# Two column passes joined into one in the MLP's seven-product units of a float32 decoder trunk

## The chip, the cores and the metric

The kernel runs on one core of a Trainium2 chip. A core has a matrix engine (TensorE, PE in the profile; its weight loads are PEld), VectorE (DVE), ScalarE (ACT), GpSimd (POOL) and SyncE (SP, which issues most transfers here). SBUF is the working memory, PSUM the banks into which PE writes and from which DVE and ACT read. The metric is the device time of one execution in microseconds (us), as the median of several runs.

## The reference

A two-layer decoder trunk in float32, 512 tokens of width 1024, batch 1. Layer 0 mixes tokens with a gated recurrence and pooling, layer 1 with a convolution module. Each layer then has cross-attention into 256 memory tokens and the gated MLP below, each with a residual add, and a final norm ends it.

```python
def conv_ffn(x, norm, w_up, dw_w, dw_b, w_down):
    h = rms_norm(x, norm) @ w_up              # 1024 -> 2 * 3072
    g = causal_dwconv(h[..., :D_FF], dw_w, dw_b)   # width 3
    u = h[..., D_FF:]
    return (jax.nn.gelu(g) * u) @ w_down      # 3072 -> 1024

for layer in range(DEPTH):
    x = x + mixer(x)                          # one kind in layer 0, another in layer 1
    x = x + cross_attn(x, mem, ...)
    x = x + conv_ffn(x, ...)
return rms_norm(x, final_norm)
```

## The kernel before

Activations lie transposed: a tile is 128 channels by 512 tokens (`T`), and X is eight such tiles. Float32 products are made of rounded parts: each operand is split into a high part (a copy by ACT into the type float32r) and a low part (what is left, a subtraction by DVE), and `mm3` (L186 to L188) runs three matmuls: high weights by high input, high weights by low input, low weights by high input. For one pair of tiles this is called a k-step below, and each matmul a pass.

In each layer's MLP the up projection has 24 units, numbered 0 to 23. Units 0 and 1 are plain. Units 2 to 23 each make one tile of the gate and one of the value by a scheme of seven products instead of eight (Strassen's in Winograd's form): weights and input are cut in 2 x 2 blocks, the tokens into two halves of 256 (`M`). `Seven` holds the input's side: the blocks B11, B21, B22 are halves of the normed input's tiles (`norm.x[c]`, a high and a low tile of 512 columns each; columns 0 to 255 of tiles 0 to 3 are B11, of tiles 4 to 7 B21, and columns 256 to 511 of tiles 4 to 7 are B22), and T1 to T4 are sums of blocks kept in eight `big` tiles, high and low apart. `Blocks` holds the weights' side: a11, a12, a22 as loaded, and s1 to s4, which are made by accumulating DMAs on POOL's queue (L825, L828, L830), then split by `high` (ACT, L815) and `low` (DVE, L822). `Seven.product` makes one product: four k-steps, so twelve passes of 256 columns.

A unit accumulates in three PSUM tiles, each a bank of which columns 0 to 255 are used. All come from the pool `main_ps` with five banks. `stat_ps` has one bank, `aux_ps` two.

- H: s1 by T1, then s4 by B22
- G: a11 by B11, then a12 by B21
- F: starts as ACT's copy of G after a11 by B11 (L928), then s2 by T2, s3 by T3, a22 by T4

On PE the order in unit c is: s1 (H), s2 (F), a12 (G), s3 (F), the down projection's 24 passes of 512 columns for an earlier group of four units, a11 of unit c + 1 (`ahead`), s4 (H), a22 (F). Partial results are read between them: u is F after s2 (ACT, L946) and F after s3 (ACT, L967); `times_r` (L887) reads G and F and multiplies by the norm's scale r; the adds of L171 read H. `gating(c)` is a generator that runs on into unit c + 1: the add of H, the multiplication by r (L905), the convolution (ACT L895, two on DVE at L898), gelu (ACT L900), the product with the value (DVE L914), and the split of the result (ACT L917, DVE L919).

The order of PE, ACT, DVE and POOL in the MLP is written out by hand (`manual_schedule`): each works through its queue in the program's order. Between the units' parts the queues of ACT and DVE also hold the splits of the next units' weights, the down weights (ACT L200, DVE L203), and ACT's copies of X into the down projection's banks and back (L855, L860); SP loads each unit's raw weights two or three units ahead. After layer 0's last unit the last group's down products are made outside a hand-written order: there a scheduler takes instructions by priority, `high_priority(n)` moves them up, and each `sum` adds into X (L866) and feeds the next norm's sum of squares (ACT L246, DVE L248), among the splits of coming weights (L166, L167).

Of the kernel before, what the change touches and what calls it, by code (L numbers as in the profile page):

```python
# [10 lines left out]
F32 = mybir.dt.float32  # L11
F32R = mybir.dt.float32r
AF = mybir.ActivationFunctionType
# [25 lines left out]

KE = 2  # L40
PARKED = 4
READY = 8
WINDOWS = (2, 4, 8, 16)

# [17 lines left out]
def trunk(ctx: ExitStack, tc: tile.TileContext, I: dict, out: list):  # L62
# [26 lines left out]
    def big_f():  # L89
        return big.tile([P, 2 * T], F32, tag="big", name=nm("big"))  # L90
# [93 lines left out]
    def mm3(ps, w, x, first, last, onto=False):  # L184
        (wh, wl), (xh, xl) = w, x
        PE.matmul(ps, wh, xh, start=first, stop=False, skip_group_check=onto)  # L186
        PE.matmul(ps, wh, xl, start=False, stop=False, skip_group_check=onto)  # L187
        return PE.matmul(ps, wl, xh, start=False, stop=last, skip_group_check=onto)  # L188
# [16 lines left out]
    def blk(w, i, n=P):  # L205
        hi, lo = (w.hi, w.lo) if isinstance(w, Piece) else w
        if isinstance(hi, list):
            hi, lo, i = hi[i // T], lo[i // T], i % T
        return hi[:, i : i + n], lo[:, i : i + n]


    class Norm:
        due = None
# [516 lines left out]
    class Seven:  # L730
# [6 lines left out]
        def __init__(self, norm, n=4):  # L737
            self.norm = norm
            self.t = [(big_r(), big_r()) for _ in range(n)]
            self.t4 = None if n == 4 else big_f()  # L740

        def fourth(self, k):
            split(self.t4[:, k * M : (k + 1) * M], *[x[:, M:] for x in self.norm.x[k]])

        def sums(self, k, between=None):

            f = [tmp_f(), tmp_f()]
            for i in range(2):
                c = k + 4 * i
                A.activation(f[i], X[c], AF.Copy, scale=col(self.norm.gain[0], self.norm.gain[1] + c))  # L750
            if between:
                between()
            (b11, b12), (b21, b22) = [(x[:, :M], x[:, M:]) for x in f]
            t13, t24 = tmp_f(), tmp_f()
            t1, t3, t2, t4 = t13[:, :M], t13[:, M:], t24[:, :M], t24[:, M:]
            V.tensor_tensor(t3, b22, b12, op=ALU.subtract)
            V.tensor_tensor(t1, b11, b12, op=ALU.subtract)
            V.scalar_tensor_tensor(t2, t3, -1.0, b11, op0=ALU.mult, op1=ALU.subtract)
            at = slice(k * M, (k + 1) * M)
            if self.t4 is not None:  # L760
                t4 = self.t4[:, at]
            V.scalar_tensor_tensor(t4, t2, -1.0, b21, op0=ALU.mult, op1=ALU.subtract)
            for (hi, _), t in zip(self.t, (t1, t2, t3, t4)):
                A.activation(hi[:, at], t, AF.Copy)
            yield
            for (hi, lo), t in zip(self.t, (t1, t2, t3, t4)):
                V.tensor_tensor(lo[:, at], t, hi[:, at].bitcast(F32), op=ALU.subtract)

        def product(self, ps, w, j, first=True):
            for c in range(4):  # L770
                if j - self.T1 == len(self.t):
                    x = blk(self.norm.x[c], M, M)
                elif j >= self.T1:
                    x = blk(self.t[j - self.T1], c * M, M)
                else:
                    x = blk(self.norm.x[c if j == self.B11 else c + 4], M if j == self.B22 else 0, M)
                mm3(ps, blk(w, c * P), x, first and c == 0, c == 3, not first)
            return ps

    class Blocks:  # L780
# [54 lines left out]
    def ffn(layer, norm, nxt, seven, pairs):  # L835
# [50 lines left out]
        def times_r(out, ps, at):  # L886
            V.tensor_tensor(out[:, at], ps, norm.r[:, at], op=ALU.mult)  # L887
# [3 lines left out]
        def gate_conv(c, g):  # L891
# [8 lines left out]
            A.activation(y, y, AF.Gelu_apprx_tanh)  # L900
            yield y

        def gating(c, g, f, u, F, H):
            add(g[:, right_half], H, u[:, :M])
            V.tensor_tensor(g[:, right_half], g[:, right_half], norm.r[:, right_half], op=ALU.mult)  # L905
# [12 lines left out]
            yield  # L918
            V.tensor_tensor(ys[c][1], y, ys[c][0].bitcast(F32), op=ALU.subtract)  # L919
# [3 lines left out]

        def ahead(c):

            G, F = main_ps()[:, :M], main_ps()[:, :M]
            m(c, G, "a11", seven.B11)
            A.activation(F, G, AF.Copy)  # L928
            return G, F

        def unit(c):

            nonlocal left, chains
            G, F = chains
# [11 lines left out]
            A.activation(u[:, :M], F, AF.Copy)  # L946
# [20 lines left out]
            A.activation(u[:, M:], F, AF.Copy)  # L967
# [6 lines left out]
            V.tensor_tensor(f[:, right_half], f[:, right_half], norm.r[:, right_half], op=ALU.mult)  # L974
            both(c + 2, "a11")
            high(c + 1, "a12")
            low(c + 1, "a12")
            if down:
                for ks in (range(GC - 1), (GC - 1,)):
                    for i in range(2):  # L980
                        down.products(i, d[i], seeded, ks)
            if c + 3 in pairs:
                pairs[c + 3].load()
            if c + 2 in pairs and c > first:
                pairs[c + 2].load_second()
            if c > second and c + 1 in downs:
                downs[c + 1].w.high()
                downs[c + 1].w.low()
            if c + 2 in downs and first < c <= CF - 2:
                downs[c + 2].load()  # L990
            high(c + 1, "s1")
            low(c + 1, "s1")
            high(c + 1, "s2")
            low(c + 1, "s2")
            if c == second:
                downs[c + 1].w.high()
                downs[c + 1].w.low()
            if down:
# [105 lines left out]
        if nxt:  # L1104
            mem = Memory(1)
            mem.operand(0)
            mem.operand(1)
            mem.outputs()
            parked = []
            for n in range(PARKED):  # L1110
                if n + 1 < C // 2:
                    downs[CF + n + 1].w = load_w(I["wdown"][(layer * NG + NG - 1) * (C // 2) + n + 1])
                parked.append(mem.key_piece(n, park=True))
            for j in range(C // 2):
                for i in range(2):
# [785 lines left out]
```

## Time and profile before

| what | value |
|---|---|
| median of 3 runs | 1429.62 us (1429.07 to 1431.03) |
| the profiled execution | 1429.09 us |
| its span, first to last instruction | 1427.3 us |
| granted TensorE clock, mean | 0.998 |
| PE busy | 1417.0 us, 8650 matmuls |
| DVE busy | 1073.2 us, 1796 instructions |
| ACT busy | 901.6 us, 1592 instructions |
| POOL busy | 317.3 us, 333 instructions |

Times of instructions are from the profiled execution and count from the start of its span. A row of a timeline gives start, duration, engine, line, operation, output and inputs by the program's names, shape and count; in brackets stands the engine's idle time before it and what ended it. The starts of neighbouring matmuls tell what each one costs, as their durations overlap.

### The profile page before, as it was taken

Reading aid. Unit: us, or ns where it says so; the run is one execution under the profiler, and the core shown is the slowest. Engines: PE = TensorE matmul, PEld = TensorE weight load, DVE = VectorE, ACT = ScalarE, POOL = GpSimd, SP = SyncE. Lnnn points to the kernel's source line nnn. Section 1 sums busy time; section 2 is a strip of 40 time slices with the busy share of each in tenths; the row PEclk is TensorE's granted clock in tenths of the full one; section 3 lists DMA queues with packets and bytes.
Section 4 is the critical chain, followed back from the end, with each engine's and each line's share of the span. In section 5 each row is a group of like instructions: output and inputs, shape, how many; then the busy total and the mean of one; then the engine's idle time right before and its main releaser. Section 6 shows DMA issues by size and latency. Waiting matters only on the chain.

```text
span 1427.3 us, 22834 instructions
## 1 busy us (share of the span) xinstructions
PE 1417.0 (99%) x8650; PEld 1262.6 (88%) x8650; DVE 1073.2 (75%) x1796; ACT 901.6 (63%) x1592; POOL 317.3 (22%) x333
## 2 busy tenths in 40 slices
PE   9999999999999999999999999999999999999998
PEld 8988888998999999999988777899889999999997
DVE  6987776778786676667798997968788676676665
ACT  7678754667565666666665557767665665666664
POOL 0011310210122222222008992011002222222211
PEclk9999999999999999999999999999999999999999
DMA  8522232544487777777442354345438777777741
GB/s 304 196 79 99 89 122 78 118 111 148 96 199 171 170 172 167 172 168 165 133 133 89 119 159 152 106 88 141 118 83 199 180 175 167 170 174 165 175 120 60
DMA packets 80031, 204.33 MB, mean 143 GB/s; under 512 B 9008, under 2 KB 9520, under 8 KB 79920
## 3 DMA queue, kind: packets, MB, share of 16 engines
q1 hardware_dynamic: 50832, 150.15, 33.0%
q0 software_dynamic: 28800, 52.44, 21.4%
q8 instruction: 68, 1.11, 0.3%
q14 instruction: 43, 0.35, 0.1%
q10 hardware_dynamic: 288, 0.27, 0.1%
HBM read 145.16 MB, written 2.10 MB: 103 GB/s over the span
## 4 chain that ended last, share of the span: by engine, by line
PE 91%; DVE 3%; POOL 2%; ACT 1%; DMA 1%; issue 1%; SPq 0%; POOLq 0%; DVEq 0%; ACTq 0%
PE mm L186 22%; PE mm L187 22%; PE mm L188 22%; PE aux L186 7%; PE aux L187 7%; PE aux L188 7%; PE mm L458 2%; DVE wlo L167 1%; DMA raw<-in_wv 1%; POOL actf L1501 1%; ACT whi L166 1%; PE aux L532 0%; POOL act L167 0%; POOL tmp L1322 0%; DMA raw<-in_pw 0%
## 5 line engine op out<-in xcount | busy, mean ns | idle before, releaser
L187 PE MATMUL mm<-act,whi 128*128 128x512 f32 (+2 forms) x1061 | 369.2, 348 | 0.3 <-DVE act L181 0.2
L186 PE MATMUL mm<-act,whi 128*128 128x512 f32 (+2 forms) x1061 | 368.8, 349 | 0.6 <-ACT act L274 0.6
L188 PE MATMUL mm<-act,wlo 128*128 128x512 f32 (+2 forms) x1061 | 368.9, 348 | 0.0
L186 PEld LDWEIGHTS mm<-act,whi 128*128 128x128 f32 x1061 | 200.5, 189 | 28.1 <-ACT act L274 1.0
L187 PEld LDWEIGHTS mm<-act,whi 128*128 128x128 f32 x1061 | 200.7, 189 | 27.4 <-DVE act L167 1.0
L188 PEld LDWEIGHTS mm<-act,wlo 128*128 128x128 f32 x1061 | 200.7, 189 | 24.9 <-DVE wlo L167 0.6
L822 DVE TENSOR_TENSOR bigr<-raw,bigr 128x512 fp32r<-128x512 f32 x176 | 120.9, 688 | 129.3 <-ACT bigr L815 125.6
L186 PE MATMUL mm<-bigr,bigr 128*128 128x256 f32 x704 | 199.4, 283 | 0.0
L187 PE MATMUL mm<-bigr,bigr 128*128 128x256 f32 x704 | 199.2, 283 | 0.0
L188 PE MATMUL mm<-bigr,bigr 128*128 128x256 f32 x704 | 199.2, 283 | 0.0
L815 ACT ACTIVATE bigr<-raw 128x512 fp32r<-128x512 f32 x176 | 109.4, 623 | 80.0 <-DVE wlo L203 75.7
L828 POOL DMA_DIRECT2D raw<-wa x100 | 87.9, 899 | 308.5 <-DVE bigr L822 208.6
L186 PE MATMUL aux<-act,whi 128*128 128x512 f32 x399 | 155.7, 390 | 0.0
L187 PE MATMUL aux<-act,whi 128*128 128x512 f32 x399 | 155.7, 390 | 0.0
L188 PE MATMUL aux<-act,wlo 128*128 128x512 f32 x399 | 155.2, 389 | 0.0
L166 ACT ACTIVATE whi<-raw 128x1024 fp32r<-128x1024 f32 (+1 forms) x95 | 96.6, 1021 | 85.2 <-PE mm L187 44.4
L186 PEld LDWEIGHTS mm<-bigr,bigr 128*128 128x128 f32 x704 | 135.1, 192 | 0.0
L188 PEld LDWEIGHTS mm<-bigr,bigr 128*128 128x128 f32 x704 | 135.2, 192 | 0.0
L187 PEld LDWEIGHTS mm<-bigr,bigr 128*128 128x128 f32 x704 | 135.2, 192 | 0.0
L825 POOL DMA_DIRECT2D raw<-raw x50 | 43.3, 866 | 367.5 <-DVE wlo L822 343.8
L167 DVE TENSOR_TENSOR wlo<-raw,whi 128x1024 fp32r<-128x1024 f32 (+1 forms) x75 | 90.4, 1211 | 19.1 <-ACT whi L166 18.5
L188 PEld LDWEIGHTS aux<-act,wlo 128*128 128x128 f32 x399 | 74.9, 188 | 15.9
(353 smaller groups left out, 3044.0 us busy)
## 6 DMA issues: line engine op xcount, KB each, us to landing
raw<-wa POOLq DMA_DIRECT2D x150, 256.0 KB, 3.4
wa<-in_wpair SPq DMA_DIRECT2D x88, 256.0 KB, 3.7
raw<-in_wpair SPq DMA_DIRECT2D x44, 512.0 KB, 3.8
big<-in_wdown SPq DMA_DIRECT2D x42, 512.0 KB, 4.5
raw<-raw POOLq DMA_DIRECT2D x50, 256.0 KB, 3.7
raw<-in_pw SPq DMA_DIRECT2D x24, 512.0 KB, 3.4
raw<-in_win SPq DMA_DIRECT2D x20, 512.0 KB, 3.3
raw<-in_wk SPq DMA_DIRECT2D x16, 512.0 KB, 3.5
```

What stands on the lines that cost most here:

```text
L166: A.activation(hi, src, AF.Copy)
L167: fetched[1] = (eng or V).tensor_tensor(lo, src, hi.bitcast(F32), op=ALU.subtract)
L186: PE.matmul(ps, wh, xh, start=first, stop=False, skip_group_check=onto)
L187: PE.matmul(ps, wh, xl, start=False, stop=False, skip_group_check=onto)
L188: return PE.matmul(ps, wl, xh, start=False, stop=last, skip_group_check=onto)
L458: PE.matmul(p, m[j], x, start=k == 0 and j == 0 and x is hi, stop=k == C - 1 and x is lo)
L815: A.activation(self.w[name][0], self.block(name), AF.Copy)
L822: V.tensor_tensor(lo, self.block(name), hi.bitcast(F32), op=ALU.subtract)
L825: G.dma_start(self.r, self.z, accum_op=ALU.add)
L828: G.dma_start(block, self.a22, accum_op=ALU.add)
L1501: G.tensor_tensor(z[:, s:], z[:, s:], f[:, s:], op=ALU.add)
```

## The change

In units 6 to 21 of each layer (`WIDE`), the products of the chains G and F run each k-step as two passes. The input's high and low parts lie side by side in one tile of 512 columns. One pass multiplies the high weights by both, into all 512 columns of the bank; the other multiplies the low weights by the high part, into the left half. The bank's right half then holds high by low, and `gather` adds the halves: ACT copies the right half out, DVE adds the left half from PSUM. H keeps three passes of 256 and takes its bank from `stat_ps` in these units. `gating` multiplies g and f by r over 512 columns at once, after the gathers. In the last k-step of a product the narrow pass comes first.

T1 to T4 are laid out side by side from the start. B11, B21 and B22 are re-laid by ACT in units 4 and 5: `put_aside` copies B22's high part out of the way, and `put_beside` moves the low parts of B11 and of B21 beside their high parts and B22's high part beside its low part, each four copies of 256 columns. In unit 7's `ahead` one more pass of 512 columns writes F's bank before ACT's copy. After layer 0's last unit the sums into X get a higher priority.

```diff
+WIDE = range(6, 22)
...
+    def parts(x):
+        return x[:, :M], x[:, M:]
+
+    def move(to, x):
+        A.activation(to, x.bitcast(F32), AF.Copy)
...
-            for (hi, _), t in zip(self.t, (t1, t2, t3, t4)):
-                A.activation(hi[:, at], t, AF.Copy)
+            both = [self.both(self.T1 + j, k) for j in range(len(self.t))]
+            for x, t in zip(both, (t1, t2, t3, t4)):
+                A.activation(x[:, :M], t, AF.Copy)
             yield
...
+        def both(self, j, c):
+            if j >= self.T1:
+                return self.t[j - self.T1][c // 2][:, c % 2 * T : (c % 2 + 1) * T]
+            return self.norm.x[c if j == self.B11 else c + 4][j == self.B22]
...
+        def put_aside(self):
+            self.aside = act_r(), act_r()
+            for c in range(4):
+                move(parts(self.aside[c // 2])[c % 2], self.norm.x[c + 4][0][:, M:])
+
+        def put_beside(self, j):
+            for c in range(4):
+                if j == self.B22:
+                    move(self.norm.x[c + 4][1][:, :M], parts(self.aside[c // 2])[c % 2])
+                else:
+                    hi, lo = self.norm.x[c if j == self.B11 else c + 4]
+                    move(hi[:, M:], lo[:, :M])
+            self.beside.add(j)
 
         def product(self, ps, w, j, first=True):
             for c in range(4):
...
+                wh, wl = blk(w, c * P)
+                if ps.shape[-1] == T:
+                    x = self.both(j, c)
+                    steps = [(ps, wh, x), (ps[:, :M], wl, x[:, :M])]
+                    for i, (to, part, by) in enumerate(steps if c < 3 else steps[::-1]):
+                        PE.matmul(
+                            to, part, by, start=first and c == 0 and i == 0, stop=c == 3 and i == 1, skip_group_check=True
+                        )
                 else:
...
+                    mm3(ps, (wh, wl), self.block(j, c), first and c == 0, c == 3, not first)
...
+        def bank(c):
+            return main_ps() if wide(c) else main_ps()[:, :M]
+
+        def gather(out, ps):
+            A.activation(out, ps[:, M:], AF.Copy)
+            add(out, ps[:, :M], out)
...
         def gating(c, g, f, u, F, H):
             add(g[:, right_half], H, u[:, :M])
-            V.tensor_tensor(g[:, right_half], g[:, right_half], norm.r[:, right_half], op=ALU.mult)
+            if wide(c):
+                V.tensor_tensor(g, g, norm.r, op=ALU.mult)
...
-            times_r(f, F, left_half)
+            if wide(c):
+                gather(f[:, left_half], F)
+                V.tensor_tensor(f, f, norm.r, op=ALU.mult)
...
         def ahead(c):
-            G, F = main_ps()[:, :M], main_ps()[:, :M]
+            G, F = bank(c), bank(c)
             m(c, G, "a11", seven.B11)
+            if c == WIDE[0] + 1:
+                PE.matmul(F, pairs[c].w["a11"][0][:, :P], seven.both(seven.B11, 0), start=True, stop=True)
             A.activation(F, G, AF.Copy)
...
-            H = main_ps()[:, :M]
+            H = (stat_ps if wide(c) else main_ps)()[:, :M]
...
             m(c, F, "s2", seven.T2, False)
+            if wide(c):
+                gather(u[:, :M], F)
...
             low(c, "s4")
-            if c > second:
+            if wide(c):
+                gather(g[:, left_half], G)
+            elif c > second:
                 times_r(g, G, left_half)
 
             m(c, F, "s3", seven.T3, False)
+            if wide(c):
+                gather(u[:, M:], F)
...
-            V.tensor_tensor(f[:, right_half], f[:, right_half], norm.r[:, right_half], op=ALU.mult)
+            if not wide(c):
+                V.tensor_tensor(f[:, right_half], f[:, right_half], norm.r[:, right_half], op=ALU.mult)
             both(c + 2, "a11")
             high(c + 1, "a12")
             low(c + 1, "a12")
+            if c == WIDE[0] - 2:
+                seven.put_aside()
+            elif c == WIDE[0] - 1:
+                seven.put_beside(seven.B21)
...
+            if c == WIDE[0] - 2:
+                seven.put_beside(seven.B11)
 
             m(c, H, "s4", seven.B22, False)
             m(c, F, "a22", seven.T4, False)
+            if c == WIDE[0] - 1:
+                seven.put_beside(seven.B22)
             left = gating(c, g, f, u, F, H)
...
-                    downs[CF + j].sum(i, ps)
+                    with tc.high_priority(URGENT):
+                        downs[CF + j].sum(i, ps)
```

More of the change, by code (lines that the diff above doesn't have):

```diff
@@ L740, in __init__ @@
             self.t4 = None if n == 4 else big_f()
+            self.beside, self.aside = set(), None
         def fourth(self, k):
@@ L762, in sums @@
             V.scalar_tensor_tensor(t4, t2, -1.0, b21, op0=ALU.mult, op1=ALU.subtract)
-            for (hi, _), t in zip(self.t, (t1, t2, t3, t4)):
-                A.activation(hi[:, at], t, AF.Copy)
+            both = [self.both(self.T1 + j, k) for j in range(len(self.t))]
+            for x, t in zip(both, (t1, t2, t3, t4)):
+                A.activation(x[:, :M], t, AF.Copy)
             yield
-            for (hi, lo), t in zip(self.t, (t1, t2, t3, t4)):
-                V.tensor_tensor(lo[:, at], t, hi[:, at].bitcast(F32), op=ALU.subtract)
+            for x, t in zip(both, (t1, t2, t3, t4)):
+                V.tensor_tensor(x[:, M:], t, x[:, :M].bitcast(F32), op=ALU.subtract)
@@ new lines, in both, with block @@
+        def both(self, j, c):
+            if j >= self.T1:
+                return self.t[j - self.T1][c // 2][:, c % 2 * T : (c % 2 + 1) * T]
+            return self.norm.x[c if j == self.B11 else c + 4][j == self.B22]
+        def block(self, j, c):
+            if j - self.T1 == len(self.t):
+                return blk(self.norm.x[c], M, M)
+            if j >= self.T1 or j in self.beside:
+                return parts(self.both(j, c))
+            if j == self.B22 and self.aside:
+                return parts(self.aside[c // 2])[c % 2], self.norm.x[c + 4][1][:, M:]
+            return blk(self.norm.x[c if j == self.B11 else c + 4], M if j == self.B22 else 0, M)
@@ L769, in product @@
         def product(self, ps, w, j, first=True):
             for c in range(4):
[L771 to L774, printed above, removed]
-                else:
-                    x = blk(self.norm.x[c if j == self.B11 else c + 4], M if j == self.B22 else 0, M)
-                mm3(ps, blk(w, c * P), x, first and c == 0, c == 3, not first)
+                wh, wl = blk(w, c * P)
@@ L901, in gate_conv, with wide @@
             yield y
+        def wide(c):
+            return c in WIDE
+        def bank(c):
[3 more added lines that the diff above has]
+            add(out, ps[:, :M], out)
         def gating(c, g, f, u, F, H):
             add(g[:, right_half], H, u[:, :M])
-            V.tensor_tensor(g[:, right_half], g[:, right_half], norm.r[:, right_half], op=ALU.mult)
+            if wide(c):
+                V.tensor_tensor(g, g, norm.r, op=ALU.mult)
+            else:
+                V.tensor_tensor(g[:, right_half], g[:, right_half], norm.r[:, right_half], op=ALU.mult)
             conv = gate_conv(c, g)
@@ L908, in gating @@
             yield
-            times_r(f, F, left_half)
+            if wide(c):
+                gather(f[:, left_half], F)
+                V.tensor_tensor(f, f, norm.r, op=ALU.mult)
+            else:
+                times_r(f, F, left_half)
             next(conv)
@@ L945, in unit @@
             u, f, g = tmp_f(), tmp_f(), tmp_f()
-            A.activation(u[:, :M], F, AF.Copy)
+            if wide(c):
+                gather(u[:, :M], F)
+            else:
+                A.activation(u[:, :M], F, AF.Copy)
             if c == first:
@@ L962, in unit @@
             low(c, "s4")
-            if c > second:
+            if wide(c):
+                gather(g[:, left_half], G)
+            elif c > second:
                 times_r(g, G, left_half)
             m(c, F, "s3", seven.T3, False)
-            A.activation(u[:, M:], F, AF.Copy)
+            if wide(c):
+                gather(u[:, M:], F)
+            else:
+                A.activation(u[:, M:], F, AF.Copy)
             add(f[:, right_half], H, u[:, M:])
```

## The prediction

> **What bounds the kernel now.** I read the page first: the share of busy time, then the chain that ended last.
>
> ```profile
> span 1427.3 us, 22834 instructions
> ...
> PE 1417.0 (99%) x8650; PEld 1262.6 (88%) x8650; DVE 1073.2 (75%) x1796; ACT 901.6 (63%) x1592; POOL 317.3 (22%) x333
> ...
> PE 91%; DVE 3%; POOL 2%; ACT 1%; DMA 1%; issue 1%; SPq 0%; POOLq 0%; DVEq 0%; ACTq 0%
> ```
>
> PE is never idle for long and 91% of the chain is matmuls, so what counts is how long a matmul holds PE until the next one starts, and whether the changed buffers make PE wait. The PE timeline of one unit of layer 1's MLP gives the first. Its columns are start, duration, engine, line, operation, names, shape.
>
> ```profile
> 1149.89 0.28 PE L186 MATMUL mm<-act,whi 128*128 128x256 f32 x1
> ...
> 1152.65 0.28 PE L188 MATMUL mm<-bigr,bigr 128*128 128x256 f32 x1
> 1152.78 0.40 PE L186 MATMUL aux<-act,whi 128*128 128x512 f32 x1
> ...
> 1158.02 0.39 PE L188 MATMUL aux<-act,wlo 128*128 128x512 f32 x1
> 1158.24 0.28 PE L186 MATMUL mm<-act,whi 128*128 128x256 f32 x1
> ```
>
> Starts are what to read, since durations overlap. From 1149.89 to 1152.78 are 24 passes of 256 columns: 2.89 / 24 = 0.1204 us each. From 1152.78 to 1158.24 are 24 passes of 512: 5.46 / 24 = 0.2275. Twice the columns cost 1.89 times as much: 0.107 us for 256 columns and a fixed 0.0133 for each pass, whatever its width. Where the widths meet the steps are the same (1152.65 to 1152.78, 1158.02 to 1158.24), so alternating them should cost nothing.
>
> The stretch of one whole unit, from the busy time by windows (length, PE, PEld, DVE, ACT, POOL, granted clock, DMA share, GB/s):
>
> ```profile
> 1147.00:1162.54 15.54, 15.54 (x110) 14.58 (x109) 10.51 (x18) 9.64 (x19) 3.30 (x4) 1.00 0.72 170
> ```
>
> 84 x 0.1204 + 24 x 0.2275 = 15.57, against 15.54 shown: the unit is back-to-back matmuls at full clock, with DVE free for a third of it and ACT for more.
>
> **The change, part by part.**
>
> **Joined passes.** A k-step of a product is three passes of 256 now (high x high, high x low, low x high): 0.361. Joined it is one of 512 and one of 256: 0.2275 + 0.1204 = 0.348. It saves 0.0133, the fixed part of one pass. Five of a unit's seven products go to the chains G and F (a11, a12; s2, s3, a22), with four k-steps each: 20 x 0.0133 = 0.267 per unit, so the unit becomes 15.30 (call it 15.3). Units 6 to 21 in two layers are 32: **-8.5 us**. The Trainium skill, page "TensorE: Matmul & The Clock Gate", section "Back-to-back issue gap", puts a warm matmul at N/2.4 ns and a fixed 2.5 ns; by that the same edit saves 640 x 2.5 ns = 1.6 us. The trace here does not agree (13.3 ns fixed), and the sum takes the trace.
>
> **Extra seeding pass** in unit 7's `ahead`: one 512-column pass per layer, nothing beside it on PE: 2 x 0.2275 = **+0.5**.
>
> **Gathers.** The low part now lies in the bank's right half and must be added. Per wide unit that adds four 256-column ACT copies less the two of u that exist already, and two net 256-column DVE adds for u; the adds for f and g take the place of two `times_r`. The multiplications by r turn from two pairs of 256 into two of 512, and ACT's copy G to F doubles its width. Durations are in the next two fences: the ACT timeline, then DVE's.
>
> ```profile
> 1150.10 0.39 ACT L946 ACTIVATE tmp<-mm 128x256 f32<-128x256 f32 x1 [2.58 <-PE mm L188]
> 1150.38 1.11 ACT L855 ACTIVATE aux<-x 128x512 f32<-128x512 f32 x2
> ...
> 1154.45 0.62 ACT L815 ACTIVATE bigr<-raw 128x512 fp32r<-128x512 f32 x1
> 1154.98 0.37 ACT L967 ACTIVATE tmp<-mm 128x256 f32<-128x256 f32 x1
> ...
> 1159.85 0.63 ACT L815 ACTIVATE bigr<-raw 128x512 fp32r<-128x512 f32 x1 [2.00 <-DVE wlo L203]
> ...
> 1162.24 0.82 ACT L895 ACTIVATE tmp<-tmp,par 128x512 f32<-128x512 f32 x1 [0.48 <-DVE tmp L905]
> ```
>
> ```profile
> 1155.19 0.68 DVE L822 TENSOR_TENSOR bigr<-raw,bigr 128x512 fp32r<-128x512 f32 x1
> 1155.80 0.42 DVE L887 TENSOR_TENSOR tmp<-mm,r 128x256 f32<-128x256 f32 x1
> 1156.13 0.41 DVE L171 TENSOR_TENSOR tmp<-mm,tmp 128x256 f32<-128x256 f32 x1
> 1156.46 0.68 DVE L822 TENSOR_TENSOR bigr<-wa,bigr 128x512 fp32r<-128x512 f32 x1
> 1157.06 0.41 DVE L974 TENSOR_TENSOR tmp<-tmp,r 128x256 f32<-128x256 f32 x1
> ...
> 1158.60 1.22 DVE L203 TENSOR_TENSOR wlo<-big,whi 128x1024 fp32r<-128x1024 f32 x1
> 1159.74 1.47 DVE L822 TENSOR_TENSOR bigr<-raw,bigr 128x512 fp32r<-128x512 f32 x2
> 1161.32 0.42 DVE L171 TENSOR_TENSOR tmp<-mm,tmp 128x256 f32<-128x256 f32 x1
> 1161.77 0.43 DVE L905 TENSOR_TENSOR tmp<-tmp,r 128x256 f32<-128x256 f32 x1
> 1162.75 0.42 DVE L887 TENSOR_TENSOR tmp<-mm,r 128x256 f32<-128x256 f32 x1 [0.55 <-PE mm L188]
> 1163.10 1.53 DVE L898 SCALAR_TENSOR_TENSOR tmp<-tmp,par,tmp 128x511 f32<-128x511 f32 x2
> ```
>
> DVE gets 2 x 0.42 (u) + (0.69 - 0.41) + (0.69 - 0.43), about 1.4: 10.5 becomes 11.9 of 15.3. ACT gets 2 x 0.38 and 0.2 for the wider copy: 9.6 becomes 10.6. By totals all of it is covered by matmuls. What totals cannot show are the two places where PE now waits for these queues sooner than before, so I walk them, in us from the start of a unit (1147.00 here). Instructions without a dependence start some 0.08 before the end of the one ahead (1155.19 + 0.68 against 1155.80); a dependent one starts 0.03 to 0.05 after it.
>
> *H in the single stat bank.* The next unit's first product (s1) writes H's bank, so it must wait for `gating`'s add of H, which today has five rotating banks behind it. The queue ahead of that add hangs on u's copy (1150.10, or 3.10 into the unit; 3.04 once two products are joined): today the add starts 11.22 later. Between them DVE gains u's second add (0.33 of issue) and a dependent start (0.13) and loses L974 (0.33). The last split (1159.74, two, ending 1161.21, its end set by L203 through ACT's 1159.85) lets DVE take the add at 11.03 after the copy now, 11.15 then: 14.19 into the unit. PE's s4 product ends at about 14.10. The add ends at 14.61, and s1 wants the bank at 15.30: **0.65 to spare, cost nothing**. ACT's copy G to F, longer by 0.2, stands behind L815 at 1159.85 and delays only the second home copy; F is wanted two products after the unit's end.
>
> *F between s2 and s3.* Today PE may write F again once ACT's 0.39 copy is done. Now ACT copies the right half, then DVE adds the left, and s3 follows only one product (a12, 1.39) after s2. DVE's queue ahead of that add, from the next unit's start: H's add -1.11 to -0.68; r over 512 columns (0.69) to +0.05; ACT's L895 (0.82) to 0.90, then f's copy to 1.19; f's add 1.22 to 1.64; r on f, 0.69, to 2.37; the two L898 (1.53) to 3.82; u's add 3.74 to 4.16, and PE can go on at about 4.20. s3 is due at 1.44 + 2 x 1.39 = **4.22**. The cover is gone to within 0.02, and my pitches are good to about 0.1. An overrun is halved as long as DVE, and not PE, is what H's add waits for (it stands 0.08 behind PE, and each stall gives DVE time). Bounds: nothing, and 0.15 per unit if every pitch is at its worst: 4.5 us over 30 units (the first of each layer has a narrow unit's gating ahead of it). I take 0.03 per unit, as the walk ends just on time: **+0.8**. The Trainium skill, "PSUM — Partial Sum Buffer", section "PSUM bank collisions raise a hardware error", says that two engines may not be in one bank at once, even in different columns; by that rule s3 has to wait for both readers of F, which adds to this wait. No row of before shows it, as ACT alone reads F between those products.
>
> **Re-laying the input's parts** (units 4 and 5): 16 ACT copies of 256 columns per layer in four groups. The nearest row is three such copies:
>
> ```profile
> 906.96 1.02 ACT L764 ACTIVATE bigr<-tmp 128x256 fp32r<-128x256 f32 x3
> ```
>
> One group of four is 1.3. Two groups go ahead of the down weights' copy (L200), into ACT's 2.00 idle ahead of 1159.85; two go ahead of L895, ahead of a 2.58 idle. Moving a group past L895 makes the gating 0.7 later, which the DVE queue has room for in a narrow unit. No DMA moves: SP's loads and POOL's accumulating copies keep their places, and their triggers (the splits) stay within 0.15. Cost **0**; without that cover, 4 groups x 1.3 x 2 = 10 at the very most. The new layout of the t tiles has the same number of copies and subtractions: 0.
>
> **Urgent sums** at the end of layer 0. DVE's and PE's timelines there:
>
> ```profile
> 731.88 1.22 DVE L167 TENSOR_TENSOR wlo<-raw,whi 128x1024 fp32r<-128x1024 f32 x1
> 733.02 1.48 DVE L248 TENSOR_TENSOR tmp<-tmp,tmp 128x512 f32<-128x512 f32 x2
> ```
>
> ```profile
> 739.97 0.49 PE L186 MATMUL mm<-act,whi 128*128 128x512 f32 x1 [0.60 <-ACT act L274]
> 740.70 0.50 PE L187 MATMUL mm<-act,whi 128*128 128x512 f32 x1 [0.23 <-DVE act L181]
> ```
>
> The norm's sum (L248) stands behind a weight split of 1.22, and PE then waits 0.83 in all for the scaled input. If the sums overtake the split, up to 0.8 goes; if the order turns so that a split is late for PE, up to 1.2 comes. I take **-0.3**.
>
> **Sum:** -8.5 + 0.5 + 0.8 - 0.3 = -7.5. The profiled execution took 1429.09, so 1421.6; the median of the runs shown is 0.5 higher, so 1422.1.
>
> **Rivals.**
> 1. *F's wait bites*: s3 stalls 0.1 to 0.2 in each wide unit. For it: 0.02 of room in the walk. Against: a stall relieves DVE, so only what is late by more than some 0.15 is paid in full. At 0.15 x 30 = 4.5 instead of 0.8: 1425.8.
> 2. *Joining saves nothing*: a 512-column pass that alternates with one of 256 takes 0.241, twice a narrow one, because the weights must be swapped in the short pass between. Then 0.5 + 0.8 - 0.3 = 1.0 is added: 1430.6, within what a measurement of this kernel can tell from no change (about 0.2%, 2.9 us). Against it: the starts above do not change where the widths meet. With the skill's 2.5 ns, the figure for this case would be 1429.0.
> 3. *Slower: H's single bank.* If DVE reaches H's add more than 0.65 later than walked, s1 waits in every unit; past 0.65 + 0.24 = 0.9 the wait exceeds the saving of a unit. At 1.2 late each unit loses 0.55: 32 x 0.55 = 17.6 against -7.5, 1439.7. For it: one bank where there were five to rotate, and DVE nearly 80% busy. Against: the add's queue hangs on ACT and L203, which gain 0.12.
>
> **How the numbers follow.** As forecast (1420.0 to 1424.2): 0.62. F's wait (1424.2 to 1427): 0.16. No measurable change, by rival 2 or by costs of the re-laying that I put at zero: 0.11. Slower: 0.08. Faster than 1420, if the junction gives all and F never waits: 0.03. The range 1419.8 to 1427.2 leaves out under two in ten. Faster by over 0.2%: 0.81; within: 0.11; slower: 0.08.
>
> **What would show it.** In the changed trace: starts of 0.2275 and 0.12 in turn in the five products and 15.3 from unit to unit; no wait of PE on DVE's L171 at the first s3 pass (a stall of 0.1 there is rival 1) or at the first s1 pass (rival 3); 16 more ACT copies per layer with PE unbroken beside them; and the gap ahead of the conformer's first passes under 0.8. The prediction is wrong if PE's steps in joined products exceed 0.348 per k-step, or if PE shows waits in units 6 to 21.

## The result and the profile after

The changed kernel's median is 1424.42 us (1423.37 to 1424.93) against 1429.7 for the kernel before: a ratio of 0.9961, with an interval of 0.9949 to 0.9974. That is 5.3 us faster, where 7.5 were forecast. The profiled execution took 1424.63, with a span of 1422.8. One run of a later kernel (units 5 to 23) was slow, 2347.5 us at a granted clock of 0.556; that kernel's median counts it, its ratio does not.

The page of the changed kernel, its first lines, its chain by engine and the largest group of joined passes (those of s2, s3 and a22):

```profile
span 1422.8 us, 21779 instructions
...
PE 1411.7 (99%) x8012; PEld 1228.3 (86%) x8012; DVE 1115.0 (78%) x1860; ACT 934.0 (66%) x1688; POOL 316.8 (22%) x333
...
PE 92%; DVE 2%; POOL 2%; DMA 1%; issue 1%; ACT 1%; SPq 0%; POOLq 0%; DVEq 0%; ACTq 0%
...
L817 PE MATMUL mm<-bigr,bigr 128*128 128x512 f32 (+1 forms) x768 | 150.6, 338 | 0.0
```

There are 638 matmuls fewer: 640 narrow passes gone, and two seeding passes added. The kernel is still bound by PE, and PE spent no time idle ahead of the joined passes (the 0.0 at the end of the last row).

The busy time by windows shows where the time went. Each row below covers ten whole units of layer 1, all of them in the changed range, from the down product of one unit to that of the tenth after it. The columns are window, length, busy time (and instructions) of PE, PEld, DVE, ACT and POOL, granted clock, DMA share, GB/s. First the kernel before:

```profile
1137.23:1292.63 155.40, 155.40 (x1082) 145.82 (x1081) 105.07 (x181) 96.45 (x181) 34.59 (x40) 1.00 0.73 170
```

Then the changed one:

```profile
1135.61:1289.06 153.45, 153.45 (x881) 135.05 (x880) 117.99 (x201) 103.90 (x201) 34.46 (x40) 1.00 0.72 172
```

A unit went from 15.540 to 15.345. It saves 0.195, where 0.267 was forecast, and PE is as full as it was. DVE gained 1.29 a unit and ACT 0.75, a little less than the 1.4 and 1.0 of the prediction.

By the starts of the same instructions, the span up to PE's last matmul divides like this (us):

| stretch | before | after |
|---|---|---|
| start to layer 0's first copy into F | 378.85 | 379.44 |
| layer 0, first to last copy into F | 312.69 | 309.84 |
| from there to the conformer's first pass | 48.43 | 48.21 |
| the conformer, to layer 1's first copy into F | 325.16 | 326.14 |
| layer 1, first to last copy into F | 312.69 | 309.81 |
| from there to PE's last matmul | 42.23 | 42.24 |

The two MLP stretches give 2.85 + 2.88 = 5.73. The other stretches moved by up to 1.0, and they moved as much among experiments that leave them alone (start 378.7 to 380.3, conformer 325.1 to 326.1). So the 5.73 is the change, and the 1.3 that the profiled execution gave back outside is not.

### The profile page after: what moved, and what is told of

The parts are those of the page before. It is cut to its first block, busy times and chain, and to the rows that moved or that the text cites. A ratio compares the mean times of both kernels' runs of the same rounds, so it can differ in the third digit from the quotient of the medians.

```text
span 1422.8 us, 21779 instructions
## 1 busy us (share of the span) xinstructions
PE 1411.7 (99%) x8012; PEld 1228.3 (86%) x8012; DVE 1115.0 (78%) x1860; ACT 934.0 (66%) x1688; POOL 316.8 (22%) x333
## 4 chain that ended last, share of the span: by engine, by line
PE 92%; DVE 2%; POOL 2%; DMA 1%; issue 1%; ACT 1%; SPq 0%; POOLq 0%; DVEq 0%; ACTq 0%
PE mm L817 16%; PE mm L187 15%; PE mm L188 15%; PE mm L189 15%; PE aux L187 7%; PE aux L188 7%; PE aux L189 7%; PE stat L187 2%; PE stat L189 2%; PE stat L188 2%; PE mm L465 2%; DMA raw<-in_wv 1%; POOL actf L1583 1%; DVE wlo L168 1%; PE aux L539 0%
## 5 line engine op out<-in xcount | busy, mean ns | idle before, releaser
L188 PE MATMUL mm<-act,whi 128*128 128x512 f32 (+2 forms) x805 | 296.8, 369 | 0.3 <-DVE act L182 0.2
L187 PE MATMUL mm<-act,whi 128*128 128x512 f32 (+2 forms) x805 | 296.6, 370 | 0.6 <-ACT act L281 0.6
L189 PE MATMUL mm<-act,wlo 128*128 128x512 f32 (+2 forms) x805 | 296.6, 368 | 0.0
L187 PEld LDWEIGHTS mm<-act,whi 128*128 128x128 f32 x805 | 151.5, 188 | 26.8 <-ACT act L281 0.9
L188 PEld LDWEIGHTS mm<-act,whi 128*128 128x128 f32 x805 | 151.7, 188 | 26.0 <-DVE act L168 1.0
L189 PEld LDWEIGHTS mm<-act,wlo 128*128 128x128 f32 x805 | 151.6, 188 | 25.1 <-DVE wlo L168 0.6
L817 PE MATMUL mm<-bigr,bigr 128*128 128x512 f32 (+1 forms) x768 | 150.6, 338 | 0.0
L817 PEld LDWEIGHTS mm<-bigr,bigr 128*128 128x128 f32 x768 | 118.3, 189 | 14.3
L172 DVE TENSOR_TENSOR tmp<-mm,tmp 128x256 f32<-128x256 f32 x194 | 77.8, 417 | 40.4 <-ACT tmp L955 37.9
L817 PE MATMUL mm<-act,whi 128*128 128x512 f32 x256 | 95.5, 396 | 0.0
L188 PEld LDWEIGHTS aux<-act,whi 128*128 128x128 f32 x399 | 74.9, 188 | 15.5
L187 PEld LDWEIGHTS aux<-act,whi 128*128 128x128 f32 x399 | 75.0, 188 | 14.2
```

Of the source, the lines that this page charges most:

```text
L172: V.tensor_tensor(out, a, b, op=ALU.add)
L817: PE.matmul(to, part, by, start=first and c == 0 and i == 0, stop=c == 3 and i == 1, skip_group_check=True)
```

## Why a joined pass saves less: the experiments

In the changed kernel, PE's timeline of one product shows the disputed steps (a11, just after the down product):

```profile
1156.40 0.39 PE L817 MATMUL mm<-act,whi 128*128 128x512 f32 x1
1156.63 0.28 PE L817 MATMUL mm<-act,wlo 128*128 128x256 f32 x1
1156.74 0.40 PE L817 MATMUL mm<-act,whi 128*128 128x512 f32 x1
1156.97 0.28 PE L817 MATMUL mm<-act,wlo 128*128 128x256 f32 x1
1157.09 0.40 PE L817 MATMUL mm<-act,whi 128*128 128x512 f32 x1
1157.33 0.40 PE L817 MATMUL mm<-act,wlo 128*128 128x256 f32 x2
1157.57 0.40 PE L817 MATMUL mm<-act,whi 128*128 128x512 f32 x1
1157.81 0.28 PE L187 MATMUL stat<-act,bigr 128*128 128x256 f32 x1
```

The product takes 1157.81 - 1156.40 = 1.41, or 0.352 per k-step, where the prediction had 0.348. The first wide pass, right behind 24 other wide ones, takes 0.23; the later ones take 0.23 to 0.24, and the narrow ones 0.11 to 0.12. Three theories could tell why. A: each change between widths costs. C: the first few wide passes behind narrow ones cost more, and then the price falls. D: a wide pass in these products costs more at all times, because of its operands. Beside them stood the wait for F.

**All wide passes of a product first, then the narrow ones** (one change of width within a product, where there were six):

```diff
-    for i, (to, part, by) in enumerate(steps if c < 3 else steps[::-1]):
-        PE.matmul(to, part, by, ...)
+    PE.matmul(ps, wh, self.both(j, c), ...)
...
+    for c in range(4):
+        _, wl = blk(w, c * P)
+        PE.matmul(ps[:, :M], wl, self.both(j, c)[:, :M], ...)
```

> Same arithmetic as the changed kernel, but in each joined product the four passes of 512 columns come first and the four of 256 after them, so the widths change twice per product instead of seven times. In the changed kernel a joined k-step takes 0.351 us, not 0.348, and a unit 15.34. Theory A (each change of width costs PE some ns): passes go back to 0.227 and 0.120, a unit to 15.28, and 32 units give 1.9 us: about 2 us below the changed kernel, ratio to before near 0.995. Theory B (the joined pass is dearer by itself, whatever runs beside it): still 15.34 per unit, no gain over the changed kernel.

Measured: 1423.36, ratio 0.9954 (0.9942 to 0.9967). Ten units by windows, and two products from PE's timeline (in this kernel L814 is the wide pass, L820 the narrow one):

```profile
1134.30:1287.76 153.46, 153.46 (x882) 135.03 (x881) 118.02 (x201) 103.89 (x201) 34.47 (x40) 1.00 0.73 173
```

```profile
1155.13 1.07 PE L814 MATMUL mm<-act,whi 128*128 128x512 f32 x4
1156.04 0.64 PE L820 MATMUL mm<-act,wlo 128*128 128x256 f32 x4
1156.51 0.28 PE L187 MATMUL stat<-act,bigr 128*128 128x256 f32 x1
...
1157.95 1.09 PE L814 MATMUL mm<-bigr,bigr 128*128 128x512 f32 x4
1158.88 0.63 PE L820 MATMUL mm<-bigr,bigr 128*128 128x256 f32 x4
1159.35 0.28 PE L187 MATMUL stat<-bigr,bigr 128*128 128x256 f32 x1
```

The unit is 15.346, as in the changed kernel, with far fewer changes of width: A falls. So does the wait for F as the reason, for nothing holds up s3 in this kernel: by unrounded starts, its weight load starts 2 to 5 ns behind the pass ahead, as elsewhere, in all 32 units. The two products tell more. Four wide passes behind the down product's 24 take 1156.04 - 1155.13 = 0.91, or 0.227 each. Four behind narrow passes take 1158.88 - 1157.95 = 0.93, or 0.2325 each; their single steps are 233, 236, 228 and 233 ns. The narrow ones take 0.47 for four, or 0.1175, in both.

**Every pass wide** (the low weights multiply both parts as well, so the low-by-low product is added; the narrow passes double in width):

```diff
-    steps = [(ps, wh, x), (ps[:, :M], wl, x[:, :M])]
+    steps = [(ps, wh, x), (ps, wl, x)]
```

> The changed kernel with the low weights also multiplied by both parts, so that a joined k-step is two passes of 512 columns and s2, a12, s3, the down passes and a11 are 56 passes of 512 in a row. It does more work than needed (the low by low term is added). Theory C (a 512-column pass costs some 232 ns only in the first five to ten passes after 256-column ones, and 227 after, whatever it computes): the passes of a12, s3 and a11 are 226 to 227 ns apart, a unit is 17.4 to 17.5 us, and the time is near 1490 us. Theory D (a pass that reads high and low side by side is dearer by itself): 232 to 235 ns in all of a12 and s3 and 17.65 per unit.

Measured: 1491.67, ratio 1.0432 (1.0413 to 1.0451). Ten units (17.43 each), and PE's timeline of the run of wide passes from s2 through a12 and s3 to the down product:

```profile
1172.65:1346.91 174.26, 174.26 (x881) 148.86 (x880) 119.78 (x201) 103.93 (x200) 34.51 (x40) 1.00 0.63 151
```

```profile
1202.04 2.00 PE L817 MATMUL mm<-bigr,bigr 128*128 128x512 f32 x8
1203.88 0.39 PE L817 MATMUL mm<-act,whi 128*128 128x512 f32 x1
...
1205.69 1.98 PE L817 MATMUL mm<-bigr,bigr 128*128 128x512 f32 x8
1207.50 0.39 PE L187 MATMUL aux<-act,whi 128*128 128x512 f32 x1
```

The first eight take 1.84, the next eight 1.81, the eight of s3 1.81. The single steps at the head of the run are 233, 236, 228, 233, 230 ns; from the sixth on they are 226 or 227, in the same products with the same operands. So C holds and D falls: a run of wide passes pays some 23 ns over its first four passes and 26 ns over five. It pays once here, however long it is. Not every run pays the same, though: in the grouped kernel the down product, behind s3's four narrow passes, cost 47 ns more than at 226.7 a pass, over its first nine.

This is where a unit's time goes, by unrounded starts, as means over 24 units of the two layers. At the prices of long runs, 0.120 and 0.2267, a unit would save 20 x (0.240 - 0.2267) = 0.267. Its wide passes cost 0.028 more than that in the kernel before, 0.158 in the changed kernel and 0.139 in the grouped one. Its narrow passes, those near a change of width, cost 0.008, 0.065 and 0.045 less. So the changed kernel saves 0.267 - 0.130 + 0.057 = 0.194 and the grouped one 0.267 - 0.111 + 0.037 = 0.193. This is bookkeeping, not a test. The wide passes of the changed kernel's joined products take 223 to 242 ns, 233.8 in the mean. Why alternating and grouping come to the same sum is not shown.

**Wide groups of neighbouring products meet** (two products take their narrow passes first). If a run pays once, joining runs has to save some 23 ns for each that goes:

```diff
+    full = [(ps, blk(w, c * P)[0], self.both(j, c)) for c in range(4)]
+    half = [(ps[:, :M], blk(w, c * P)[1], self.both(j, c)[:, :M]) for c in range(4)]
+    steps = half + full if j in (self.T2, self.T3) else full + half
```

> The changed kernel with each joined product's passes in two groups, ordered so that the wide groups meet: s2 and s3 run four passes of 256 and then four of 512, the others 512 first. Theory C (the first five passes of 512 after passes of 256 cost 233, 236, 228, 233, 230 ns, later ones 227): s2 with a12, and s3 with the down passes and a11, pay this 25 ns once instead of twice, some 0.025 us per unit, 15.32. But s3 is then due 0.03 earlier, and DVE's add of F leaves PE's weight load nothing to spare, so part or all of it may come back as a wait ahead of s3: 15.32 to 15.35. Against theory C: the passes behind a met group are 232 again.

Measured: 1423.75, ratio 0.9958 (0.9944 to 0.9971).

```profile
1135.20:1288.51 153.31, 153.31 (x882) 135.45 (x881) 118.08 (x201) 104.00 (x201) 34.48 (x40) 1.00 0.72 171
```

15.331 over these ten units: a third of the 0.046 came. The rest went into the wait for F: the second pass of s3, a narrow one that elsewhere takes 120 ns, took 149 in the mean, and from 118 to 203.

**The same, and F is freed sooner**: the second step of g's convolution is issued behind u's add, where it stood ahead of it, so DVE comes to that add earlier.

```diff
-def gate_conv(c, g):
+def gate_conv(c, g, apart=False):
...
+        if apart and s == 1:
+            yield y
...
+if wide(c):
+    next(conv)
```

> As e11, and DVE does the second of the two convolution steps (L942) after u's add instead of before it, so that F is free some 0.2 us sooner; gelu on ACT starts about 0.2 later. Theory (F's wait is what takes back the 0.025): no wait at s3, the weight load ahead of it at its usual lead, a unit at 15.31 to 15.32, about 1 us below the changed kernel. Rival (ACT's later gelu sets back the weights): longer units, with PE waiting for the splits of s3 or s4.

Measured: 1422.82, ratio 0.9953 (0.9941 to 0.9966): 7.2 below the kernel before in the same runs and the best median of all. Its interval overlaps with the changed kernel's; that it is faster rests on its units:

```profile
1135.32:1288.32 153.00, 153.00 (x881) 135.21 (x880) 117.97 (x200) 104.77 (x201) 34.45 (x40) 1.00 0.73 173
```

```profile
1162.83 0.74 DVE L941 SCALAR_TENSOR_TENSOR tmp<-tmp,par,tmp 128x511 f32<-128x511 f32 x1
1163.75 0.43 DVE L172 TENSOR_TENSOR tmp<-mm,tmp 128x256 f32<-128x256 f32 x1 [0.18 <-ACT tmp L956]
1164.09 0.74 DVE L941 SCALAR_TENSOR_TENSOR tmp<-tmp,par,tmp 128x510 f32<-128x510 f32 x1
```

The unit is 15.300 in every unit, 0.046 under the grouped one, as two runs less at 23 ns each would give. In detail, by unrounded starts, its wide passes cost 0.060 less and its narrow ones 0.013 more, so the 23 ns is a mean. On DVE, u's add stands between the two steps of the convolution and now waits for ACT's copy alone. In both layers' MLP stretches the saving is 6.58 us (309.35 and 309.45), against 5.73 for the change.

**The same over units 5 to 23** in place of 6 to 21:

```diff
-WIDE = range(6, 22)
+WIDE = range(5, 24)
```

> As e13, with joined passes in units 5 to 23 instead of 6 to 21 (the re-laying in units 3 and 4). Three more joined units per layer at 0.2 us each: 1.2 us below e13, some 7.5 us below before. If the re-laying in units 3 and 4, where ACT also prepares other weights, is not hidden, unit 3 or 4 gets longer instead.

Measured: 1428.94, ratio 0.9992 (0.9983 to 1.0001). The three units more gave their 0.24 each, but the ends took more. PE's waits (engine, operand, line, then engine and line waited for; us in total, times, longest):

```profile
PE stat L305 <- DVE actf L1601: 1.8, 1, 1.8
PE mm L187 <- ACT act L281: 1.5, 1, 1.5
...
PE mm L187 <- ACT mm L995: 0.9, 1, 0.9
PE aux L357 <- DVE act L334: 0.9, 1, 0.9
```

The stretch from layer 0's last copy into F to the conformer's first pass took 49.77, against 48.62 in the run before this one, and PE was idle in it for 0.9 and 1.5, close to its end. The conformer took 328.02 against 326.04. Of this, 1.5 is a lower clock: after that idle time the granted clock was 0.50, and passes of 512 columns took 0.43, until 742.9; the conformer's first 18 passes took 4.96, against 3.43 at a clock of 1.00. The windows row of that time:

```profile
739.50:742.50 3.00, 3.00 (x9) 2.54 (x10) 3.00 (x6) 1.81 (x3) 0.00 (x0) 0.50 0.03 12
```

In layer 1's first units, where the re-laying now lies in units 3 and 4, PE stood still for 0.3 to 1.1 at a time, longest for ACT's copy into F (L995). So the re-laying costs nothing where it lies in the changed kernel, and it seems to cost something one unit earlier, though no run moves it alone. Whether the longer stretch ahead of the conformer comes from the wide last units alone, no run separates.

## The parts forecast at nothing, and the wait for F

**Only the re-laying and the new layout** (no unit is wide, no seeding pass; the products keep three passes, the urgent sums stay):

```diff
-    return c in WIDE
+    return False
```

> The new layout of the t tiles, the 16 copies per layer in units 4 and 5 and the urgent sums, but all products in three passes of 256 columns and no seeding pass. Theory: the re-laying is hidden in ACT's idle time, so units take 15.54 and the MLP stretches 312.7 us as before; total within 0.5 us of before. Rival: the copies delay ACT's later work and show as PE idle in units 4 to 6, up to 10 us in all.

Measured: 1429.34, ratio 0.9994 (0.9984 to 1.0003). The MLP stretches are 312.68 and 312.69, as before to 0.01: nothing, as predicted.

**Half the units** (`WIDE = range(6, 14)`):

> Joined passes in units 6 to 13 only, 16 units instead of 32. If the gain is a saving of 0.197 us per joined unit, the two MLP stretches together lose 16 x 0.197 - 0.47 = 2.7 us against before instead of 5.7, and unit 14 on takes 15.54 again. If a part of the gain came from the new layout or the ends, the two would not stand in that ratio.

Measured: 1426.38, ratio 0.9972 (0.9963 to 0.9981). The MLP stretches give 1.29 + 1.32 = 2.61; 16 units at 0.195 less two seeding passes are 2.65. The saving goes by the unit.

**H with its five rotating banks again:**

```diff
-    H = (stat_ps if wide(c) else main_ps)()[:, :M]
+    H = main_ps()[:, :M]
```

> The changed kernel with H back in the five rotating banks of the main pool. Theory: the single bank is free 0.7 us before s1 writes it again, so it costs nothing and a unit is 15.34 with either, the time within 0.5 us of the changed kernel. Rival: s1 waits for the single bank; then this run has shorter units.

Measured: 1424.25, ratio 0.996 (0.9945 to 0.9976), unit 15.345. The single bank costs nothing.

**Without the urgent sums**, and **the kernel before with the urgent sums alone:**

```diff
-    with tc.high_priority(URGENT):
-        downs[CF + j].sum(i, ps)
+    downs[CF + j].sum(i, ps)
```

> The changed kernel with the sums at the end of layer 0 at their old priority; all else as changed. Theory: the priority brought little (the gap ahead of the conformer's first pass hardly differs, 48.43 us from the last copy G to F to that pass before and 48.21 after), so the time is within 0.3 us of the changed kernel. Rival: the other order made the conformer longer (325.2 us before, 326.1 after from its first pass to layer 1's first copy); then this run is 0.7 to 1 us faster than the changed kernel and the conformer's stretch is 325.2 again.

> The kernel before with only the higher priority of the sums at the end of layer 0. Theory: no difference that can be told from before (within 0.5 us), as the changed kernel with and without it lay within the spread of runs. Rivals: 0.8 us shorter if the wait ahead of the conformer goes, 1.2 longer if a split is late for PE.

Measured: 1423.78, ratio 0.9956 (0.9944 to 0.9969), and 1430.09, ratio 1.0002 (0.9993 to 1.001). The junction took 47.97 and 47.85, in the spread of 47.6 to 48.6 that kernels with and without the priority show. The -0.3 cannot be seen.

**u's add done twice.** The first goes into columns that are overwritten later, so only time is added: F stays in use some 0.4 longer.

```diff
-    gather(u[:, :M], F)
+    A.activation(u[:, :M], F[:, M:], AF.Copy)
+    add(u[:, M:], F[:, :M], u[:, :M])
+    add(u[:, :M], F[:, :M], u[:, :M])
```

> The changed kernel with DVE's add of F after s2 done twice (the first result is overwritten), so F is read 0.33 us longer. In the changed kernel that add ends 4.07 us into the unit and s3 is due at 4.24. Theory (F's bank is the next wait, with some 0.13 to spare): the second add ends at 4.40, PE could go on at 4.45, an overrun of 0.21; DVE stands 0.09 behind PE at H's add, so each unit gets 0.10 to 0.13 longer, 15.46, and the time 3 to 4 us above the changed kernel. Rival (DVE has room, PE does not wait for it): 15.34, no difference.

Measured: 1438.2, ratio 1.0061 (1.0049 to 1.0074): 13.8 more than the changed kernel, where an overrun was expected to be halved. PE's waits of the whole span and ten units by windows:

```profile
PE mm L817 <- DVE tmp L172: 6.7, 30, 0.2
```

```profile
1142.42:1300.60 158.18, 155.97 (x882) 134.93 (x881) 123.14 (x211) 103.92 (x200) 34.48 (x40) 1.00 0.70 167
```

The unit is 15.818, or 0.47 longer, and each is stalled. DVE's two adds, s3's first pass, and the weight loads there:

```profile
1171.55 0.88 DVE L172 TENSOR_TENSOR tmp<-mm,tmp 128x256 f32<-128x256 f32 x2
```

```profile
1171.95 0.40 PE L817 MATMUL mm<-act,whi 128*128 128x512 f32 x1
1172.58 1.30 PE L817 MATMUL mm<-bigr,bigr 128*128 128x512 f32 x6 [0.22 <-DVE tmp L172]
```

```profile
1171.84 0.19 PEld L817 LDWEIGHTS mm<-act,whi 128*128 128x128 f32 x1
1172.54 0.65 PEld L817 LDWEIGHTS mm<-bigr,bigr 128*128 128x128 f32 x4 [0.52 <-ACT aux L899]
```

The adds end at 1172.43, the weights of s3 start to load at 1172.54, and the pass starts at 1172.58, 0.15 after the adds. From the last pass of a12 that is 0.62, where 0.24 is usual: 0.38 lost, and the step behind it takes 307 ns where some 233 are usual, 0.07 more. So of the 0.41 by which F comes free later all is paid but the room of some 0.03, and the slow step behind the restart as well. It isn't halved, because DVE doesn't catch up in the next unit:

```profile
1164.94 1.48 DVE L866 TENSOR_TENSOR bigr<-raw,bigr 128x512 fp32r<-128x512 f32 x2
1166.74 0.42 DVE L172 TENSOR_TENSOR tmp<-stat,tmp 128x256 f32<-128x256 f32 x1 [0.32 <-PE stat L189]
```

H's add, the second row, stands idle for 0.32 until PE's s4 has ended. DVE is early there, and it is PE that is late. In the prediction's walk the same add hung on DVE's queue.

## Why the prediction was right, and where its sum was off

**What bounds the kernel, and the sign:** right. PE stayed unbroken through units 6 to 21, and what was saved are fixed parts of passes.

**Joined passes, -8.5:** this is the term that was mis-sized. It measured 32 x 0.195 = -6.2. The step that failed is the price of a wide pass as a mean over a run of 24, with "where the widths meet the steps are the same". The kernel before already showed it otherwise, in rows left out between those that were quoted (the second and the fifth pass of the down product):

```profile
1153.01 0.40 PE L187 MATMUL aux<-act,whi 128*128 128x512 f32 x1
...
1153.70 0.39 PE L187 MATMUL aux<-act,whi 128*128 128x512 f32 x1
```

The first four steps, from 1152.78, take 0.92 as rounded, and 0.930 by the unrounded starts (1152.775 to 1153.705): 0.2325 each, where the run's mean is 0.2278. The joined products consist of such heads only. In the changed kernel a joined k-step takes 233.8 + 117.6 = 351.3 ns in the mean (before rounding), where three passes before took 359.7: 20 x 8.4 ns is 0.168. H's narrow passes and the down product, 48 passes that each cost about 0.5 ns less than before, bring 0.026 more, and together this is 0.194. The prediction named steps above 0.348 per k-step as a sign that it is wrong; by that sign this term is wrong.

A smaller part of the miss is the reading. From starts rounded to 0.01 came 0.1204 for a narrow pass and 0.2275 for a wide one; the unrounded starts of the same passes give 0.1200 and 0.2278. The fixed part is then 12.2 ns in place of 13.3, and a unit's saving 0.244 in place of 0.267. That is 0.7 of the 2.3 us that the term lacks; what the changes of width cost in net is the other 1.6.

The rule of the Trainium skill, "TensorE: Matmul & The Clock Gate", section "Back-to-back issue gap", a fixed 2.5 ns, which the section gives for an isolated matmul, would have given 0.05 a unit; the traces show 0.195.

**Seeding pass, +0.5:** right. Unit 7 took 15.573 and 15.578 in the two layers, 0.23 more than the units after it.

**F's wait, +0.8** (0.03 in each of 30 units is 0.9, so the term has a slip of 0.1): it cost at most 0.2. In 32 units the step to s3's first pass was 235 to 242 ns, 238 in the mean, where 236 is undisturbed. The walk ended at the right place by luck, through two errors that cancelled. u's add ended 4.07 into the unit, not 4.16, but an s3 that is held up starts 0.15 after it (the doubled add shows this), not 0.04. These rows are of the unit whose s1 starts at 1160.65:

```profile
1164.30 0.42 DVE L172 TENSOR_TENSOR tmp<-mm,tmp 128x256 f32<-128x256 f32 x1
```

```profile
1164.77 0.55 PEld L817 LDWEIGHTS mm<-bigr,bigr 128*128 128x128 f32 x3
```

```profile
1164.89 1.57 PE L817 MATMUL mm<-bigr,bigr 128*128 128x512 f32 x8
```

The add ends at 1164.72, its release reaches PE's weight load at 1164.77, and s3 starts at 1164.89, 4.24 into the unit (4.22 forecast). By the 0.15 of the doubled add, PE could have gone at 1164.87: the room was 0.02, as said. The bounds were not right: "overruns are halved" and "0.15 per unit at worst" fall by the doubled add, which paid 0.47 for 0.41. As soon as PE is late, H's add waits for PE and not for DVE's queue, so a stall gives DVE no time. The rule of the Trainium skill that the prediction named here ("PSUM — Partial Sum Buffer", section "PSUM bank collisions raise a hardware error") isn't tested by this: s3's first pass writes the very columns that the add reads. Two hundredths of a microsecond stood between the forecast and a wait in each unit. How much a small lateness costs, the kernel where the wide groups meet shows: 0.03 in the mean.

**H, the re-laying:** right, at nothing each. **Urgent sums, -0.3:** not to be seen, so neither right nor wrong.

**Sum:** -6.2 + 0.5 = -5.7, against 5.73 in the MLP stretches. The median lies 2.3 above the forecast: the joined passes lack 2.3, F's wait of 0.8 did not come, the 0.3 of the urgent sums cannot be seen, and some 0.5 is in stretches that move by up to 1.0 without the change. That the total is again 2.3 is chance. The median lies inside the band that rival 1 was given (1424.2 to 1427), yet not by rival 1's way: PE shows no wait there. Rivals 2 and 3 did not occur. Rival 2 was half right, as the wide pass is dearer beside a narrow one, by some 6 ns in place of 13; its reason, a swap of the weights, no run tests.

## What to carry to other kernels

The price of an instruction in a long run of its kind is not its price in a short run: take it from the first few behind another kind, where the trace shows them. A small difference of two prices needs starts that are finer than 0.01 us, or a much longer stretch. Where two widths alternate, put the wide ones of neighbouring products together; here that was worth 0.046 of 15.35 in each unit, once the wait that it uncovered was moved away as well. A wait that ends just in time has to be priced in full for each bit of lateness, and the next restart with it, unless what follows in the waiting queue is shown to have room.

## What was not expected of the hardware

Wide passes behind narrow ones took 233, 236, 228, 233 and 230 ns, and 226 or 227 from the sixth on, at a granted clock of 1.00 throughout; in one place of the grouped kernel it was the first nine. The narrow pass right behind a long run of wide ones took 113 ns, where 120 is usual. What causes it stays open; no run tells.

The wait of a pass for a bank is taken at its weight load. Undisturbed, that load starts some 3 ns behind the start of the pass ahead. Where it is held up in the changed kernel, it starts 0.05 after the add that reads the bank has ended. It may come as late as some 0.12 before its own pass at no cost, as it did in the changed kernel; in the kernel where the wide groups meet it came 0.08 before in the mean, and the step behind it took 149 ns for 120.

And after PE had been idle for 0.9 and 1.5 within 3 us, the granted clock was 0.50 for some 3 us (the run with units 5 to 23).
